# A decoder layer on one core: raw x transposed as it lands, the norm applied as a row, conditioning weights in smaller first pieces on three engines

## The chip, the cores and the metric

The kernel runs on one core of a Trainium2 chip. The metric is the device time of one execution in microseconds, the median of several runs. One run is also recorded by the hardware profiler; its span is the time from the first to the last recorded instruction. The engines are named as in the profile: PE (matrix products), PEld (its weight loads), DVE (vectors), ACT (scalar functions and copies), POOL (GpSimd) and SP, on whose queue nearly all DMAs of this kernel are issued.

## What is computed

One layer of a conditioned decoder with 512 positions and 1024 channels, in float32. Only its beginning is touched by the change: a norm without its gain, a modulation by a conditioning vector c, and the first columns of one wide projection. What follows (two attentions, an output projection, a gated MLP) stays.

```python
def rms_norm(x, gain):
    xf = x.astype(jnp.float32)
    y = xf * lax.rsqrt(jnp.mean(xf * xf, axis=-1, keepdims=True) + NORM_EPS)
    return (y * gain.astype(jnp.float32)).astype(x.dtype)
...
    mod = (jax.nn.silu(c) @ w_ada + b_ada)[:, None, :]
    shift_a, scale_a, gate_a, shift_f, scale_f, gate_f = jnp.split(mod, 6, axis=-1)

    h = rms_norm(x, attn_norm) * (1.0 + scale_a) + shift_a
    (nq, nkc, nvc, nks, nvs, nkw, nvw, ngate,
     cq, ckv, kr, bgate) = jnp.split(h @ w_in, IN_OFFSETS, axis=-1)
...
    x = x + gate_a * ((g_a * o_a + g_b * o_b) @ w_o)
    h = rms_norm(x, ffn_norm) * (1.0 + scale_f) + shift_f
...
    return x
```

## The kernel before

Products are kept exact in float32 by splitting each factor into a rounded high part and the rest: `split` (L82 to L84) makes the high part on ACT (L83) and the low part on DVE (L84), and `mm3` makes three matmuls on PE (L87), high by high, high by low, low by high. Names ending in h and l are such halves: wh and wl of a weight piece, hTh and hTl of h. PSUM banks go by letters, psG, psS, psT, psO, psF.

A tile framework orders the program. It takes instructions by a priority and by an estimate of when each can start, and then fixes a queue for each engine, which is worked off strictly in order; each DMA on SP's queue carries one of eight semaphores in turn, so that a DMA waits until the one eight places ahead has landed. The order within a queue is therefore the scheduler's and not that of the source.

The first stage (phase 1, from L409) goes so. x comes in eight pieces of 256 KB (L417). Each gives a sum of squares, on ACT (L437) or DVE (L434); two positions' sums at a time become 1/rms on POOL (`rstd`, L135). `x_half` (L444) scales x in place by that (ACT L447, DVE L449), transposes it on PE (L453) and copies the transposed piece xnT out of PSUM on ACT (L455). Channels then stand on partitions, in eight blocks of 128, k = 0 to 7.

For the modulation, `mod_acc(j)` (L462) loads, at every second j, eight pieces of w_ada of 256 KB, the shift and scale columns of two blocks, and adds them up, each times one entry per partition of silu(c), on DVE (`gemv_step`, L120 the first, L122 the others). `mod_cols` (L473) sums the result over partitions by a little matmul with ones (psT) and makes the columns mS (shift, L477) and mA (1 + scale times gain, L480).

`prep(k)` (L500) calls both, loads two pieces of w_in (408 and 384 columns, called wr1 and wr2), issues the late loads whose turn it is (`late_load`, L494; the table LATE says which go with which k), and makes h = xnT times mA plus mS on ACT (L507), hTh on ACT and hTl on DVE. The late loads are small tables for later: rowsB, the gain row of cq, tabs (832.5 KB), the gain row of ckv, rowg, cmp_w2, md (64 KB of the mask table), and two more rows. The k loop (L515) multiplies: for each k 12 matmuls of 408 columns into psG, psG, psS, psS and 9 of 512 columns into psO, psF and a psT. This is a k-step, named k0 to k7 below.

After the loop come the cq norm and gates (L539 to L552), a second group of columns (L555 to L565; again psG, psG, psS, psS and psF, which must be free first), the compressed-branch inputs kc and vc from psO, psF and psT (L569 to L582, products with tabs on DVE, which free those banks), and the compression. Two small DVE instructions that belong to later work are placed by the scheduler within this stage: rowg scaled (L617) and md cast into maskr (L619).

## Time and profile before

| what | value |
|---|---|
| device time, median of 3 runs | 950.85 us (950.5 to 951.32) |
| span of the profiled execution | 947.3 us |
| PE busy | 914.3 us (97%) |
| DVE busy | 690.8 us (73%) |
| ACT busy | 511.0 us (54%) |
| POOL busy | 51.1 us (5%) |
| moved by DMA | 113.06 MB, mean 119 GB/s |

Busy times are of the whole span; a share of it says little of a single stage, which is why the rows further down go by stretches and by single instructions. A timeline row gives start, length, engine, line, output and inputs, and in brackets how long the engine had stood idle and what released it. Matmuls are pipelined: the distance between two starts tells their pace better than their lengths do.

### The profile page before, as it was taken

What the parts mean: (1) busy time and instruction counts of PE and PEld (TensorE: products, weight loads), DVE (VectorE), ACT (ScalarE), POOL (GpSimd) and SP (SyncE); (2) the same over time, 40 slices, a digit from 0 to 9 for tenths busy, and PEclk for the clock granted to TensorE, in tenths of its full rate; (3) what the DMA queues carried; (4) which work ended last, traced back from release to release, by engine and by line L of the source; (5) the groups of instructions that cost most, each with busy time, mean ns of one, the idle gap of its engine ahead of it and who ended that gap; (6) DMA issues with size and microseconds to landing.
All of it is one profiled execution on the core that took longest, in us unless ns stands there. A gap on an engine that the chain in (4) does not pass through costs nothing.

```text
span 947.3 us, 15181 instructions
## 1 busy us (share of the span) xinstructions
PE 914.3 (97%) x5271; PEld 801.2 (85%) x5271; DVE 690.8 (73%) x1513; ACT 511.0 (54%) x1241; POOL 51.1 (5%) x57
## 2 busy tenths in 40 slices
PE   3999899999999999999999999999999999999998
PEld 2899788889889998888889899988888888888886
DVE  6967979787977779688967788797787666622423
ACT  5556758566676557558766655445444444422221
POOL 1000101001000001001001010000000000000000
PEclk9999999999999999999999999999999999999999
DMA  9945682441331253341214265263363333333421
GB/s 298 341 112 145 180 232 82 134 136 35 115 87 34 57 170 101 101 128 43 56 46 134 75 189 150 76 175 107 95 183 101 93 97 100 94 96 101 143 91 44
DMA packets 135778, 113.06 MB, mean 119 GB/s; under 512 B 7514, under 2 KB 118678, under 8 KB 135702
## 3 DMA queue, kind: packets, MB, share of 16 engines
q1 hardware_dynamic: 134934, 110.00, 39.4%
q0 software_dynamic: 768, 2.11, 0.7%
q8 instruction: 41, 0.67, 0.3%
q14 instruction: 35, 0.29, 0.1%
HBM read 109.98 MB, written 2.10 MB: 118 GB/s over the span
## 4 chain that ended last, share of the span: by engine, by line
PE 87%; ACT 4%; DVE 4%; DMA 3%; issue 1%; SPq 0%; POOL 0%; DVEq 0%; ACTq 0%
PE psG L87 43%; PE psS L87 23%; PE psO L87 8%; PE psF L87 4%; PE psT L87 4%; PE psT L783 2%; DMA wr<-in_w_in_dram 1%; DVE wl L84 1%; ACT Pt L760 1%; DMA wr<-in_cmp_v_w_dram 1%; ACT wh L83 1%; DMA ada<-in_w_ada_dram 1%; DMA x<-in_x_dram 1%; ACT sq L223 1%; PE psT L808 0%
## 5 line engine op out<-in xcount | busy, mean ns | idle before, releaser
L83 ACT ACTIVATE wh<-wr 128x512 fp32r<-128x512 f32 (+3 forms) x304 | 186.7, 621 | 289.5 <-PE psS L87 95.0
L84 DVE TENSOR_TENSOR wl<-wr,wh 128x512 fp32r<-128x512 f32 (+3 forms) x304 | 203.6, 676 | 155.4 <-ACT wh L83 148.4
L87 PE MATMUL psG<-hTh,wh 128*128 128x512 f32 x192 | 76.5, 398 | 1.0 <-DVE qr L328 1.0
L87 PE MATMUL psG<-hTh,wl 128*128 128x512 f32 x192 | 76.3, 397 | 0.1
L87 PE MATMUL psG<-hTl,wh 128*128 128x512 f32 x192 | 76.3, 397 | 0.0
L87 PE MATMUL psS<-h2l,wh 128*128 128x512 f32 (+1 forms) x184 | 68.3, 371 | 0.0
L87 PE MATMUL psS<-h2h,wl 128*128 128x512 f32 (+1 forms) x184 | 68.2, 371 | 0.0
L87 PE MATMUL psG<-h2h,wh 128*128 128x512 f32 (+1 forms) x184 | 68.2, 372 | 0.0
L87 PE MATMUL psG<-h2h,wl 128*128 128x512 f32 (+1 forms) x184 | 68.2, 371 | 0.0
L87 PE MATMUL psG<-h2l,wh 128*128 128x512 f32 (+1 forms) x184 | 68.1, 371 | 0.0
L87 PE MATMUL psS<-h2h,wh 128*128 128x512 f32 (+1 forms) x184 | 68.0, 370 | 0.0
L760 ACT ACTIVATE Pt<-psS,nm 128x128 f32<-128x128 f32 (+2 forms) x96 | 51.1, 534 | 25.8 <-DVE nm L755 20.1
L83 ACT ACTIVATE PTh<-psT 128x384 fp32r<-128x384 f32 (+1 forms) x72 | 36.5, 528 | 22.4 <-PE psT L783 22.2
L84 DVE TENSOR_TENSOR PTl<-psT,PTh 128x384 fp32r<-128x384 f32 (+1 forms) x72 | 42.1, 597 | 8.7 <-ACT PTh L83 8.1
L122 DVE SCALAR_TENSOR_TENSOR acc<-wr,csil,acc 128x512 f32<-128x512 f32 x60 | 44.8, 747 | 2.7 <-DMA wr<-in_w_ada_dram 1.5
L87 PEld LDWEIGHTS psG<-hTh,wh 128*128 128x128 f32 x192 | 36.2, 188 | 7.6 <-PE psS L87 0.7
L87 PEld LDWEIGHTS psG<-hTh,wl 128*128 128x128 f32 x192 | 36.1, 188 | 7.1 <-DVE wl L84 0.5
L87 PEld LDWEIGHTS psG<-hTl,wh 128*128 128x128 f32 x192 | 36.1, 188 | 6.4
L87 PE MATMUL psG<-wh,hTh 128*128 128x256 f32 (+2 forms) x128 | 37.5, 303 | 2.5 <-ACT hTh L83 1.4
L87 PEld LDWEIGHTS psG<-h2h,wl 128*128 128x128 f32 x184 | 34.7, 189 | 6.0
L87 PEld LDWEIGHTS psS<-h2l,wh 128*128 128x128 f32 x184 | 34.7, 189 | 6.0
L87 PEld LDWEIGHTS psS<-h2h,wh 128*128 128x128 f32 x184 | 34.7, 188 | 6.0
(431 smaller groups left out, 2593.8 us busy)
## 6 DMA issues: line engine op xcount, KB each, us to landing
wr<-in_w_up_dram SPq DMA_DIRECT2D x88, 256.0 KB, 3.0
wr<-in_w_ada_dram SPq DMA_DIRECT2D x64, 256.0 KB, 2.9
wr<-in_w_in_dram SPq DMA_DIRECT2D x48, 256.0 KB, 3.0
wr<-in_w_down_dram SPq DMA_DIRECT2D x44, 256.0 KB, 2.6
ada<-in_w_ada_dram SPq DMA_DIRECT2D x32, 256.0 KB, 5.4
wr<-in_w_o_dram SPq DMA_DIRECT2D x32, 256.0 KB, 3.0
wr<-in_w_in_dram SPq DMA_DIRECT2D x32, 128.0 KB, 3.6
wr<-in_cmp_k_w_dram SPq DMA_DIRECT2D x16, 256.0 KB, 3.7
```

The source lines that it names most:

```text
L83: act.activation(hi, src, AF.Copy)
L84: vec.tensor_sub(lo, src, f(hi))
L87: ins = pe.matmul(o, lhsT, rhs, start=start, stop=stop, skip_group_check=True)
L122: vec.scalar_tensor_tensor(acc, w, csil[:, k:k + 1], acc, op0=ALU.mult, op1=ALU.add)
L223: act.activation(sq[:, 0:n], b, AF.Square, accum_out=dst)
L760: act.activation(Pt[:, off[x2]:off[x2] + nt[x2]], Sb[x2], AF.Exp, bias=nm[:, x2:x2 + 1], scale=-1.0, accum_out=sums[:, x2:x2 + 1])
L783: pe.transpose(tr[:, e * P:(e + 1) * P], Pt[:, o:o + P], ident)
```

## The change

x is loaded column half first, and each transposed block is made from raw x as soon as its pieces have landed (`x_chunk`, into the banks T, S, G in turn). 1/rms is computed once for all positions, laid out as a row over positions, the same on every partition: four diagonal matrices times ones on PE, copied into rrow. h becomes xT times mA times rrow on DVE; hTh is its rounded sum with mS on ACT, and hTl the rest, on DVE.

The modulation goes by MOD_GROUPS. Blocks 0 and 1 get eight pieces of 128 KB each (rows of 512 bytes); the groups at 2, 4 and 6 keep eight pieces of 256 KB, of which the odd ones are scaled in place on ACT and added up on POOL, the even ones added up on DVE as before, and one DVE add joins the two. LATE sends rowsB, the cq row and tabs later. The code ahead of and behind this is as it was, with line numbers shifted (L617 and L619 are L636 and L638 after).

```diff
-LATE = (0, 1, 1, 1, 2, 2, 2, 3, 3, 4, 5, 6, 7, 8, 9, 9, 9)
-X_ACT = ((0, 0, 1, 1), (1, 1, 1, 1))
+LATE = (0, 0, 0, 0, 0, 1, 2, 2, 3, 3, 4, 5, 6, 7, 8, 9, 9)
+MOD_GROUPS = {0: 1, 1: 1, 2: 2, 4: 2, 6: 2}
...
-        x8 = [p1.tile([P, 4, 512], F32, name=f"x{t}", tag="x8", bufs=2) for t in range(2)]
-        xt = [[x8[t // 2][:, (t % 2) * 2 + i, :] for i in range(2)] for t in range(NT)]
+        x8 = [p1.tile([P, 4, 512], F32, name=f"x{i}", tag="x8", bufs=2) for i in range(2)]
         qs = [slot("q", f"qs{i}") for i in range(4)]
         rowsA = p1.tile([64, P], F32, name="rowsA")
         dma(rowsA, vec_a)
-        for t in range(NT):
-            for i in range(2):
-                dma(xt[t][i], x[t * P:(t + 1) * P, i * 512:(i + 1) * 512])
+        for i in range(2):
+            for t in range(NT):
+                dma(x8[i][:, t, :], x[t * P:(t + 1) * P, i * 512:(i + 1) * 512])
...
+        xT = []
+
+        def x_chunk(k):
+            tr = bank("TSG"[k % 3])
+            for t in range(NT):
+                pe.transpose(tr[:, t * P:(t + 1) * P], x8[k // 4][:, t, (k % 4) * P:(k % 4 + 1) * P], ident)
+            xk = slot("KV", f"xT{k}") if k < 6 else slot("KS", f"xT{k}")[:, 0:512]
+            act.activation(xk, tr, AF.Copy)
+            xT.append(xk)
...
+                if (t + i) % 2:
                     scr = pj.tile([P, 512], F32, name="scr", tag="t2")
-                    vec.tensor_tensor_reduce(scr, xt[t][i], xt[t][i], 1.0, 0.0, ALU.mult, ALU.add, ssh[:, t, i:i + 1])
+                    vec.tensor_tensor_reduce(scr, x8[i][:, t, :], x8[i][:, t, :], 1.0, 0.0, ALU.mult, ALU.add,
+                                             ssh[:, t, i:i + 1])
                 else:
                     scr = pj.tile([P, 512], F32, name="scr", tag="qg")
-                    act.activation(scr, xt[t][i], AF.Square, accum_out=ssh[:, t, i:i + 1])
-            if t % 2:
-                t2 = slice(t - 1, t + 1)
-                vec.tensor_add(ssx[:, t2], ssh[:, t2, 0], ssh[:, t2, 1])
-                rstd(rsx[:, t2], ssx[:, t2], D, [P, 2])
-        xnT = []
-
-        def x_half(i):
-            for t in range(NT):
-                if X_ACT[i][t]:
-                    act.activation(xt[t][i], xt[t][i], AF.Copy, scale=rsx[:, t:t + 1])
+                    act.activation(scr, x8[i][:, t, :], AF.Square, accum_out=ssh[:, t, i:i + 1])
+            for k in range(4 * i, 4 * i + 4):
+                x_chunk(k)
...
+        rsx = sm.tile([P, NT], F32, name="rsx")
+        rstd(rsx, ssx, D, [P, NT])
+        dg = pj.tile([P, 512], F32, name="dg", tag="qn")
+        for t in range(NT):
+            vec.tensor_scalar(dg[:, t * P:(t + 1) * P], ident, rsx[:, t:t + 1], None, op0=ALU.mult)
+        rb = bank("F")
+        for t in range(NT):
+            mm(rb[:, t * P:(t + 1) * P], ones, dg[:, t * P:(t + 1) * P], t == 0, True)
+        rrow = p1.tile([P, 512], F32, name="rrow")
+        vec.tensor_copy(rrow, rb)
...
+        def mod_acc(j):
+            if j not in MOD_GROUPS:
+                return
+            n = MOD_GROUPS[j]
+            w = 2 * n * P
+            accs = [slot("U", "acc")[:, 0:w], None]
+            first = [True, True]
+            for k in range(KD):
+                a = slot("ml", "ada")[:, 0:w]
+                dma(a.rearrange("p (s n) -> p s n", s=2),
+                    w_ada[k * P:(k + 1) * P, 0:2 * D].rearrange("p (s n) -> p s n", s=2)[:, :, j * P:(j + n) * P])
+                e = int(n > 1 and k % 2)
+                if e:
+                    act.activation(a, a, AF.Copy, scale=csil[:, k:k + 1])
+                    if first[e]:
+                        accs[e] = a
+                    else:
+                        pool.tensor_tensor(accs[e], accs[e], a, op=ALU.add)
                 else:
-                    vec.tensor_scalar(xt[t][i], xt[t][i], rsx[:, t:t + 1], None, op0=ALU.mult)
-            for k in range(4 * i, 4 * i + 4):
-                tr = bank("T")
-                for t in range(NT):
-                    pe.transpose(tr[:, t * P:(t + 1) * P], xt[t][i][:, (k % 4) * P:(k % 4 + 1) * P], ident)
-                xk = slot("KV", f"xnT{k}") if k < 6 else slot("KS", f"xnT{k}")[:, 0:512]
-                act.activation(xk, tr, AF.Copy)
-                xnT.append(xk)
-
-        x_half(0)
-
-        ACC = {}
-
-        def mod_acc(j):
-            if j % 2 == 0:
-                acc = slot("U", "acc")
-                for k in range(KD):
-                    a = slot("ml", "ada")
-                    dma(a.rearrange("p (s n) -> p s n", s=2),
-                        w_ada[k * P:(k + 1) * P, 0:2 * D].rearrange("p (s n) -> p s n", s=2)[:, :, j * P:(j + 2) * P])
-                    gemv_step(acc, a, k, True)
-                for i in range(2):
-                    ACC[j + i] = [acc[:, s * 256 + i * P:s * 256 + (i + 1) * P] for s in range(2)]
+                    gemv_step(accs[e], a, k, first[e])
+                first[e] = False
+            acc = accs[0]
+            if n > 1:
+                vec.tensor_add(acc, acc, accs[1])
+            for i in range(n):
+                ACC[j + i] = [acc[:, (s * n + i) * P:(s * n + i + 1) * P] for s in range(2)]
...
-            act.activation(h, xnT[k], AF.Identity, scale=mA[:, k:k + 1], bias=mS[:, k:k + 1])
+            vec.scalar_tensor_tensor(h, xT[k], mA[:, k:k + 1], rrow, op0=ALU.mult, op1=ALU.mult)
             hh, hl = slot("hT", f"hTh{k}", F32R), slot("hT", f"hTl{k}", F32R)
-            split(hh, hl, h)
+            act.activation(hh, h, AF.Identity, bias=mS[:, k:k + 1])
+            vec.scalar_tensor_tensor(hl, h, mS[:, k:k + 1], f(hh), op0=ALU.add, op1=ALU.subtract)
             hTh.append(hh)
             hTl.append(hl)
 
         prep(0)
-        x_half(1)
```

The change moves instructions on the engines as the scheduler decides. Three places follow. The numbers in the names are the program's, they differ from kernel to kernel.

DVE around h of k6: before, in a row (wr_597 and wr_603 are the pieces of w_in for k6, wr_644 and wr_650 those for k7; hTl_613 is that of k6, hTl_659 that of k7).

```order
L480 TENSOR_TENSOR mA<-bp,colA 128x1
L84 TENSOR_TENSOR wl<-wr_597,wh 128x408
L84 TENSOR_TENSOR wl<-wr_603,wh 128x384
L84 TENSOR_TENSOR hTl_613<-h,hTh_612 128x512
L617 TENSOR_SCALAR rowg<-rowg 128x64
L477 TENSOR_TENSOR mS<-psT,colA 128x1
L479 SCALAR_TENSOR_TENSOR bp<-psT,colA 128x1
L480 TENSOR_TENSOR mA<-bp,colA 128x1
L619 CAST maskr<-qs_113 128x128
L84 TENSOR_TENSOR wl<-wr_644,wh 128x408
L84 TENSOR_TENSOR hTl_659<-h,hTh_658 128x512
L84 TENSOR_TENSOR wl<-wr_650,wh 128x384
```

DVE at the same place after the change (wr_634 and wr_640 are the pieces for k6, wr_680 those for k7; xT_198 and hTl_649 are of k6).

```order
L84 TENSOR_TENSOR wl<-wr_634,wh 128x408
L636 TENSOR_SCALAR rowg<-rowg 128x64
L496 TENSOR_TENSOR mS<-psT,colA 128x1
L498 SCALAR_TENSOR_TENSOR bp<-psT,colA 128x1
L84 TENSOR_TENSOR wl<-wr_640,wh 128x384
L499 TENSOR_TENSOR mA<-bp,colA 128x1
L638 CAST maskr<-qs_113 128x128
L526 SCALAR_TENSOR_TENSOR h<-xT_198,mA,rrow 128x512
L529 SCALAR_TENSOR_TENSOR hTl_649<-h,mS,hTh_648 128x512
L84 TENSOR_TENSOR wl<-wr_680,wh 128x408
```

The cast of md (L619, now L638) stood behind hTl of k6, and now stands ahead of h of k6, which has come to DVE.

ACT around hTh of k1: before (wr_362 and wr_368 are the pieces for k2; h<-xnT_177 and hTh_304 are of k1).

```order
L83 ACTIVATE wh<-wr_290 128x408
L83 ACTIVATE wh<-wr_296 128x384
L83 ACTIVATE wh<-wr_362 128x408
L507 ACTIVATE h<-xnT_177,mS,mA 128x512
L83 ACTIVATE wh<-wr_368 128x384
L83 ACTIVATE hTh_304<-h 128x512
L507 ACTIVATE h<-xnT_184,mS,mA 128x512
```

ACT at the same place after the change (wr_390 and wr_396 are the pieces for k2; the L478 are scalings of odd pieces of w_ada, those around hTh_328 of group 4; hTh_328 is of k1, hTh_404 of k2).

```order
L478 ACTIVATE ada<-ada,csil 128x512 x3
L83 ACTIVATE wh<-wr_314 128x408
L83 ACTIVATE wh<-wr_320 128x384
L83 ACTIVATE wh<-wr_390 128x408
L478 ACTIVATE ada<-ada,csil 128x512 x2
L83 ACTIVATE wh<-wr_396 128x384
L528 ACTIVATE hTh_328<-h,mS 128x512
L478 ACTIVATE ada<-ada,csil 128x512 x2
L528 ACTIVATE hTh_404<-h,mS 128x512
```

Ahead of hTh of k1 there are now the scalings of two pieces of the group that is needed for k4 and k5; h is no longer in this queue.

SP around the first pieces: before (wr_232 and wr_238 are the pieces of w_in for k0, wr_290 to wr_368 those for k1 and k2).

```order
L417 DMA x_112<-in_x_dram 128x512 x4
L467 DMA ada<-in_w_ada_dram 128x2x256 x8
L112 DMA wr_232<-in_w_in_dram 128x408
L112 DMA wr_238<-in_w_in_dram 128x384
L494 DMA rowsB<-in_vec_b_dram 76x128
L467 DMA ada<-in_w_ada_dram 128x2x256 x8
L112 DMA wr_290<-in_w_in_dram 128x408
L112 DMA wr_296<-in_w_in_dram 128x384
L112 DMA wr_362<-in_w_in_dram 128x408
L112 DMA wr_368<-in_w_in_dram 128x384
```

SP at the same place after the change (wr_264 and wr_270 are the pieces of w_in for k0, wr_314 to wr_396 those for k1 and k2).

```order
L416 DMA x_112<-in_x_dram 128x512 x4
L474 DMA ada<-in_w_ada_dram 128x2x128 x16
L474 DMA ada<-in_w_ada_dram 128x2x256
L112 DMA wr_264<-in_w_in_dram 128x408
L474 DMA ada<-in_w_ada_dram 128x2x256
L112 DMA wr_270<-in_w_in_dram 128x384
L474 DMA ada<-in_w_ada_dram 128x2x256 x6
L112 DMA wr_314<-in_w_in_dram 128x408
L112 DMA wr_320<-in_w_in_dram 128x384
L112 DMA wr_390<-in_w_in_dram 128x408
L112 DMA wr_396<-in_w_in_dram 128x384
L474 DMA ada<-in_w_ada_dram 128x2x256 x8
```

The pieces of w_in for k0 now stand behind sixteen half-size pieces and one or two full ones of w_ada.

## Rows read from the trace of the kernel before

**Rows 1.** Page, busy time and share of the span: PE and the others
```profile
PE 914.3 (97%) x5271; PEld 801.2 (85%) x5271; DVE 690.8 (73%) x1513; ACT 511.0 (54%) x1241; POOL 51.1 (5%) x57
```

**Rows 2.** Busy us by stretch, then granted clock, DMA share, GB/s (engines as named)
```profile
core 0: us, PE busy (x) PEld busy (x) DVE busy (x) ACT busy (x) POOL busy (x), PEclk, DMA share, GB/s
0.00:25.00 25.00, 10.40 (x45) 8.13 (x46) 17.63 (x45) 14.43 (x29) 3.04 (x8) 1.00 0.93 302
25.00:30.00 5.00, 4.66 (x28) 4.15 (x27) 4.72 (x13) 3.23 (x6) 0.00 (x0) 1.00 1.09 351
10.00:45.00 35.00, 28.34 (x140) 24.52 (x140) 32.83 (x72) 21.24 (x38) 1.70 (x2) 1.00 1.07 347
0.00:50.00 50.00, 33.64 (x167) 29.27 (x168) 39.16 (x96) 27.64 (x51) 3.04 (x8) 1.00 0.98 320
50.00:55.00 5.00, 5.00 (x29) 4.62 (x28) 1.73 (x7) 1.20 (x3) 0.00 (x0) 1.00 0.55 151
```

**Rows 3.** Timeline of PE: start, us, line, output and inputs, [idle before <-releaser]
```profile
29.73 0.46 PE L87 MATMUL psG<-wh,hTh 128*128 128x408 f32 x1
...
45.04 0.45 PE L87 MATMUL psG<-wh,hTh 128*128 128x408 f32 x1 [1.41 <-ACT hTh L83]
...
54.62 0.34 PE L87 MATMUL psG<-wh,hTh 128*128 128x408 f32 x1
...
58.88 0.34 PE L87 MATMUL psG<-wh,hTh 128*128 128x408 f32 x1
...
70.98 0.50 PE L87 MATMUL psF<-hTh,wh 128*128 128x512 f32 x1 [0.35 <-DVE a L575]
```

**Rows 4.** Timeline of DVE at the late small loads
```profile
54.09 0.20 DVE L617 TENSOR_SCALAR rowg<-rowg 128x64 f32<-128x64 f32 x1 [2.46 <-DMA rowg<-in_row_g_dram]
...
54.97 0.23 DVE L619 CAST maskr<-qs 128x128 bf16<-128x128 f32 x1 [0.37 <-DMA qs<-in_tab_dram]
```

**Rows 5.** Instructions by line and shape, 0 to 60 us: busy us, mean ns of one
```profile
L122 DVE SCALAR_TENSOR_TENSOR acc<-ada,csil,acc 128x512 f32<-128x512 f32 x28 | 21.0, 749 | 0.7 <-DMA ada<-in_w_ada_dram 0.3
...
L507 ACT ACTIVATE h<-xnT,mS,mA 128x512 f32<-128x512 f32 x8 | 6.5, 810 | 6.8 <-DVE mA L480 4.3 <-DVE hTl L84 2.4
...
L83 ACT ACTIVATE hTh<-h 128x512 fp32r<-128x512 f32 x8 | 5.0, 624 | 0.1
...
L83 ACT ACTIVATE wh<-wr 128x384 fp32r<-128x384 f32 x8 | 4.1, 517 | 1.2 <-DMA wr<-in_w_in_dram 0.6 <-PE psT L87 0.6
...
L447 ACT ACTIVATE x<-x,rsx 128x512 f32<-128x512 f32 x6 | 3.9, 712 | 2.8 <-POOL rsx L135 2.8
```

**Rows 6.** DMA queue: packets, MB, share of 16 engines, 68 to 70 us (512-byte rows)
```profile
q1 hardware_dynamic: 511, 0.25, 48.9%
```

**Rows 7.** The same, 11 to 17 us (conditioning weights, rows of 1 KB)
```profile
q1 hardware_dynamic: 2106, 2.14, 109.2%
```

**Rows 8.** SP's queue, waits of 0 to 60 us: total, times, longest
```profile
SPq L494 <- DMA tabs<-in_tab_dram: 2.4, 1, 2.4
```

**Rows 9.** Timeline of POOL
```profile
1.02 0.29 POOL masks.py:199 TENSOR_SCALAR_AFFINE_SELECT ident<-ident 128x128 f32<-128x128 f32 x1
...
106.42 1.02 POOL L135 TENSOR_TENSOR r<-ms,neghalf 128x4 f32<-128x4 f32 x1 [20.10 <-DVE ms L132]
113.31 2.59 POOL L135 TENSOR_TENSOR r<-ms,neghalf 128x4 f32<-128x4 f32 x1 [5.88 <-DVE ms L132]
```

**Rows 10.** Timeline of DVE beside the operation at 113.31
```profile
113.13 0.70 DVE L84 TENSOR_TENSOR wl<-wr,wh 128x512 fp32r<-128x512 f32 x1
...
114.33 0.70 DVE L84 TENSOR_TENSOR wl<-wr,wh 128x512 fp32r<-128x512 f32 x1
114.94 0.29 DVE L650 SCALAR_TENSOR_TENSOR th<-th,psT 128x128 f32<-128x128 f32 x1
```

More of the change, by code (lines that the diff above doesn't have):

```diff
@@ L118, in gemv_step @@
     def gemv_step(acc, w, k, init):
-        if k == 0 and init:
-            vec.tensor_scalar(acc, w, csil[:, 0:1], None, op0=ALU.mult)
+        if init:
+            vec.tensor_scalar(acc, w, csil[:, k:k + 1], None, op0=ALU.mult)
         else:
@@ L127, in gemv @@
             dma(w, w_ada[k * P:(k + 1) * P, c0:c0 + 512])
-            gemv_step(acc, w, k, init)
+            gemv_step(acc, w, k, init and k == 0)
     def rstd(o, ss, n, shape):
@@ L433, in tile_hybrid_layer @@
+        ssh = sm.tile([P, NT, 2], F32, name="ssh")
+        for i in range(2):
+            for t in range(NT):
+                if (t + i) % 2:
                     scr = pj.tile([P, 512], F32, name="scr", tag="t2")
-                    vec.tensor_tensor_reduce(scr, xt[t][i], xt[t][i], 1.0, 0.0, ALU.mult, ALU.add, ssh[:, t, i:i + 1])
+                    vec.tensor_tensor_reduce(scr, x8[i][:, t, :], x8[i][:, t, :], 1.0, 0.0, ALU.mult, ALU.add,
+                                             ssh[:, t, i:i + 1])
@@ L460, in tile_hybrid_layer @@
+        rb = bank("F")
+        for t in range(NT):
+            mm(rb[:, t * P:(t + 1) * P], ones, dg[:, t * P:(t + 1) * P], t == 0, True)
+        rrow = p1.tile([P, 512], F32, name="rrow")
+        vec.tensor_copy(rrow, rb)
         ACC = {}
         def mod_acc(j):
[L463 to L471 removed]
+            if j not in MOD_GROUPS:
[15 more added lines that the diff above has]
+                        pool.tensor_tensor(accs[e], accs[e], a, op=ALU.add)
+                else:
+                    gemv_step(accs[e], a, k, first[e])
[5 more added lines that the diff above has]
+                ACC[j + i] = [acc[:, (s * n + i) * P:(s * n + i + 1) * P] for s in range(2)]
```

8 lines of the change are left out of this document (2 added, 6 removed).

## The prediction

> **What bounds the kernel now.** I read the page's busy shares first: PE is busy 97% of the span [rows 1]. So the question is never how much work DVE or ACT has in all, but where PE waits, and whether a later start of the first stage's PE work is made good anywhere. The changed instructions all lie in the first 75 us, so I went next to stretches of that time. In the first 50 us the DMA engines are full (16.0 MB at 320 GB/s, share 0.98) and DVE is busy 39 of 50 us; from 50 us the loads thin out (151 GB/s) and DVE has 1.7 us of work in 5, while PE is busy 5.00 of 5.00 [rows 2]. So until 50 us loads and DVE set the pace, and PE after that.
>
> Third, PE's timeline at the first matmul of a k-step, the psG<-wh,hTh one. k1 starts at 29.73, k4 at 45.04 after a gap of 1.41, k6 at 54.62, k7 at 58.88; PE next waits at 70.98, for 0.35, at the F bank of the second group [rows 3]. k1 to k6 is 24.89 us, 23.5 without the gap, 4.7 a step with the little matmuls of the conditioning between; k6 to k7 is 4.26; k7 to the F bank 12.10. Behind the F bank the two kernels queue the same instructions in the same order on PE, which is full, so a shift of that matmul is a shift of the end. The forecast is therefore the start of k6 and k7 afterwards, and what the second group adds.
>
> Fourth, what stands in front of h and hTh on DVE and ACT. Before, DVE stood 2.46 us for rowg (54.09) and 0.37 for the small table md (the cast at 54.97) [rows 4]. Nothing on PE noticed: these stand between hTl of k6 and the work of k7, and ACT makes h.
>
> **The change part by part.**
>
> *Raw x transposed, norm as a row.* Six scalings of x on ACT (0.71 each) and two on DVE go [rows 5], and the transposes no longer wait for the norm. Four small diag products, four matmuls and a copy come. All of it lies ahead of k0. k0 needs its own two w_in pieces, which now stand behind sixteen half-size and one or two full conditioning pieces. It may start a little earlier than before; I give it no value, since PE then waits for k1 anyway, and 4.3 us of k0 end well ahead of that.
>
> *Smaller first pieces.* 2.10 MB now come in rows of 512 bytes. In a stretch that moved 0.25 MB in 511 packets the queue was busy 48.9% of 16 engines for 2 us, 30.6 ns a packet; in one of 1 KB packets 2106 took 109.2% of 6 us, 49.8 ns [rows 6, 7]. Two halves cost 61.2 against 49.8, and 2048 of them over 16 engines 1.46 us: every load behind is 1.5 us later. Lower bound 0 (halves at half the price). The total of bytes up to md stays the same.
>
> *k1.* On ACT, hTh of k1 now stands behind two scalings of group 4's pieces and the wh that follows (order list). Ahead of the fourth piece of group 4 stand x, the first three groups, three steps of w_in and four pieces, 2.10+2.10+2.10+1.22+1.05 = 8.57 MB; before, 7.55 MB had moved by 25 us and 351 GB/s followed [rows 2], so byte 8.57 is at 27.9, and with the 1.5 at 29.4. Then a scaling 0.71, wh 0.52 and hTh 0.62 [rows 5] and small gaps: k1 at 31.5, 1.8 us later than before. From there at 23.5 us to k6: 55.0, if nothing else holds.
>
> *h on DVE, and the loads of md.* This is the term that decides. h for a step costs 0.75 on DVE in place of 0.81 on ACT, hTl keeps its form [rows 5]; eight steps are balanced by half of the conditioning products leaving DVE, so as a sum of work this is nothing. But the order list has h of k6 on DVE directly behind the cast that waits for md, and rowg a few instructions ahead of it. A DMA that no PE work depended on until k7 now stands ahead of k6. What is queued behind the cast: h, hTl, both wl of k7, its columns and its h; who waits: hTh of k6 on ACT, then PE.
>
> When does md land? Before, at about 54.95. Byte-bound: what moved in 50 to 55 us is 0.755 MB, 2.2 us at 350 GB/s, so 52.2 and with the slower halves 53.7. At the old pace with the halves on top: 56.5. The old pace had SP stand 2.4 us until the big table tabs had landed [rows 8]; now tabs is issued later, after the w_in of k7, and the small loads follow it directly, so that wait should go but tabs lands later. I take the middle, 55.1, for want of a row that decides. Then cast 0.23, h 0.75, hTh 0.62 and three hand-overs of about 0.05: k6 at 56.85, against 54.62: **+2.23**. It hides a k1 as late as 33.3 (56.85 less 23.5), so the 1.8 of k1 costs nothing more, and the old 1.41 gap ahead of k4 may come or go without effect. For md at 53.7 and 56.5 the term is +0.8 and +3.6.
>
> k7 follows k6 by 4.26: from md DVE needs cast, h, hTl, two wl, columns and h, some 4 us, and hTh another 0.65, while PE has 1.75 + 4.26 = 6.0 us from md.
>
> *Second group.* In k7 all products with hTh now come first and those with hTl after, so psO closes after 12 matmuls of 0.185 and 5 of 0.227 (a step is 12 and 9 of them, 4.26), at 3.35 us, where 12 and 3 made 2.9. DVE's products with the tables on psO and psF end the wait of the F bank, and DVE is back to back from there. **+0.45**; at best 0, if the banks that close together let DVE run on.
>
> Sum: span 947.3 + 2.23 + 0.45 = 950.0. The median of the runs lies 3.55 us above this span, so the time is **953.5**.
>
> *POOL's adds.* Nine new 128x512 adds, three in each of groups 2, 4 and 6, then one DVE add that waits for them. No row shows such an add; a 128x128 select took 0.29 on POOL, four times that is 1.17, an estimate [rows 9]. Three of them lie beside DVE's own four products of 0.75 and the loads, so in the sum I set them at nothing. The Trainium skill, page "GPSIMD Engine Reference", section "3.1 Elementwise — side-by-side cycle accounting", gives 4497 ns for an add of 2048 elements; a quarter of that, an estimate from that page, is 1.12 us, and the sum by it would be the same. If the cover is gone this becomes a rival, below.
>
> **The rivals.**
>
> *A: POOL and DVE shut each other out.* At 113.31 a small POOL operation took 2.59 us, where the same one took 1.02 at 106.42. Over it DVE ran three two-input operations on SBUF back to back (0.70 each, the first at 113.13, the last at 114.33), then one that reads PSUM at 114.94; 113.31 + 2.59 = 115.90 is 0.96 after that, the operation's own length [rows 9, 10]. So POOL got nothing until DVE let go. DVE's conditioning products, its wl, h and hTl are nearly all of that kind, and DVE is busy 33 of the 35 us from 10 to 45 [rows 2]. Then a group's adds, 3 x 1.17 = 3.5 us, run only when DVE stands still for them. In group 2 that puts h of k1 3.5 us back, k1 at 35.0 and k6 at 58.5, 1.65 above the forecast. Two steps of DVE work per later group are 0.48 + 3 x 0.75 + 0.69 + 2 x 3.1 = 9.6 us, 13.1 with the adds, against 2 x 4.7 on PE: one such pair uncovered adds 3.7. So 955.2 to 958.9, say 957. Against it: from 45 us DVE has room, and it waits for loads between pieces. The Trainium skill, page "SBUF — State Buffer", section "Who interferes with whom", says a DVE instruction with two SBUF inputs contends with a GpSimd instruction that reads SBUF, and that the one that comes second fully blocks; the row at 113.31 agrees (2.59 against 1.02).
>
> *B: no change.* md lands byte-bound at 53.7 and the banks close in time: 947.3 + 0.8 + 0 to 0.45 + 3.55 = 951.7 to 952.1. For it: the loads were full before 50 us. Against: the last small loads must still queue behind 0.85 MB of tabs.
>
> *C: faster.* One mechanism: the loads of the second half run ahead. If ACT's scalings and POOL's adds free the conditioning buffers earlier, so that SP is never held, and the halves cost nothing, k1 would start at 28 and md land by 50.5, a saving of the old 1.41 gap as well: k6 at 51.5 to 52.2, 2.4 to 3.1 earlier, time 948 to 949. It decides only if md lands before about 52.4 (k6 at 54.2 or earlier). Against it: 16.7 MB at 350 GB/s do not fit in ahead of that.
>
> *D: only k0 and k1 matter.* If the scheduler's order did not bind, that is md landed early but ACT's scalings hold each hTh as at k1, k6 would be at 55.0 to 56, 951.7 to 952.7; it is not told apart from B by the time.
>
> Of the clock: the granted clock is 1.00 in all these rows [rows 2], so no row prices a lower one; k0 at twice its length would still end ahead of k1.
>
> **How the numbers follow.** About 0.2%, 1.9 us, is what a measurement of this kernel can tell from no change: same is 948.95 to 952.75. The forecast, k6 behind md, 952.2 to 955.2 round 953.5: 0.45, of which a tenth lies in same. A: 0.20, all slower. B and D: 0.25, same for the greater part. C: 0.08, mostly faster. Something worse in the same direction (loads as late as 56.5 and contention): 0.02. That makes faster 0.08, same 0.28, slower 0.64. The range reaches down past B to 950.3 and up into A to 957.5.
>
> **What would show it.** Right: DVE's cast waits at about 55 for qs<-in_tab, its h for k6 follows, and PE has a gap of 1.5 to 2.5 us ahead of k6 that ends with hTh; k1 at 31 to 32; the F bank 12.5 us behind k7. A would show POOL's adds far over 1.2 us and DVE's add on two accumulators (L488) waiting for POOL for microseconds. B would show md landed by 54. Wrong altogether: a gap ahead of k6 that ends with another releaser, or none; a k1 as late as 35; or PE's later work shifting by another amount than the F bank.

## The result and the profile after

The changed kernel takes 958.08 us (median of 4 runs, 957.54 to 958.45), the kernel before 950.67 beside it; the ratio of the runs on record is 1.0083, with a 95% interval of 1.0069 to 1.0097 (the two medians alone give 1.0078). It is slower by 7.4 us, where 2.7 were forecast, and the time lies 0.6 us above the range.

PE's timeline of the changed kernel, at the first matmul of a k-step and at the second group, which answers to [rows 3] (start, us, line, output and inputs, [idle before <-releaser]):

```profile
22.86 0.71 PE L87 MATMUL psG<-wh,hTh 128*128 128x408 f32 x1 [3.49 <-ACT hTh L528]
...
35.17 0.71 PE L87 MATMUL psG<-wh,hTh 128*128 128x408 f32 x1 [1.94 <-ACT hTh L528]
...
41.39 0.34 PE L87 MATMUL psG<-wh,hTh 128*128 128x408 f32 x1
...
52.49 0.46 PE L87 MATMUL psG<-wh,hTh 128*128 128x408 f32 x1 [1.62 <-ACT hTh L528]
...
61.99 0.44 PE L87 MATMUL psG<-wh,hTh 128*128 128x408 f32 x1
...
71.98 0.38 PE L87 MATMUL psG<-wh,hTh 128*128 128x320 f32 x1 [0.95 <-ACT sq L563]
```

Set beside the kernel before, with the F bank and the first matmul of the compression (psO) behind it:

| start, us | k0 | k1 | k2 | k3 | k4 | k6 | k7 | second group | F bank | compression |
|---|---|---|---|---|---|---|---|---|---|---|
| before | 23.50 | 29.73 | 34.13 | 38.40 | 45.04 | 54.62 | 58.88 | 63.17 | 70.98 | 83.63 |
| after | 22.86 | 35.17 | 41.39 | 46.01 | 52.49 | 61.99 | 66.43 | 71.98 | 79.68 | 92.22 |
| later by | -0.64 | 5.44 | 7.26 | 7.61 | 7.45 | 7.37 | 7.55 | 8.81 | 8.70 | 8.59 |

Three steps make nearly the whole of it: 5.4 us up to k1, 1.8 from k1 to k2, and 1.3 between k7 and the second group. Of the 1.8, 1.29 is the pace of k1's first eight matmuls (2.88 us up to the first psO product, 1.59 before), and 0.36 a little matmul pair of the conditioning that now lies within this step. From k2 to k7 only 0.3 is added; the old gap of 1.41 ahead of k4 is there again, as 1.62. The span grows from 947.3 to 955.8, as much as the compression is late, so the shift is handed on to the end.

k1 waited for hTh, and hTh on ACT for h, which is DVE's now. ACT's row of it, then DVE's and POOL's timelines around h of k1:

```profile
34.39 0.72 ACT L528 ACTIVATE hTh<-h,mS 128x512 fp32r<-128x512 f32 x1 [2.15 <-DVE h L526]
```

```profile
24.42 4.90 DVE L122 SCALAR_TENSOR_TENSOR acc<-ada,csil,acc 128x256 f32<-128x256 f32 x3
...
30.20 0.68 DVE L488 TENSOR_TENSOR acc<-acc,ada 128x512 f32<-128x512 f32 x1
...
32.36 0.14 DVE L496 TENSOR_TENSOR mS<-psT,colA 128x1 f32<-128x1 f32 x1
...
32.60 0.97 DVE L499 TENSOR_TENSOR mA<-bp,colA 128x1 f32<-128x1 f32 x1
33.60 0.75 DVE L526 SCALAR_TENSOR_TENSOR h<-xT,mA,rrow 128x512 f32<-128x512 f32 x1
...
36.20 1.25 DVE L499 TENSOR_TENSOR mA<-bp,colA 128x1 f32<-128x1 f32 x1
...
39.95 0.69 DVE L488 TENSOR_TENSOR acc<-acc,ada 128x512 f32<-128x512 f32 x1 [1.18 <-POOL ada L482]
```

```profile
23.79 4.98 POOL L482 TENSOR_TENSOR ada<-ada 128x512 f32<-128x512 f32 x3 [9.52 <-ACT ada L478]
31.91 1.65 POOL L482 TENSOR_TENSOR ada<-ada 128x512 f32<-128x512 f32 x1 [3.14 <-DMA ada<-in_w_ada_dram]
35.86 4.06 POOL L482 TENSOR_TENSOR ada<-ada 128x512 f32<-128x512 f32 x2 [2.31 <-DMA ada<-in_w_ada_dram]
...
45.70 3.00 POOL L482 TENSOR_TENSOR ada<-ada 128x512 f32<-128x512 f32 x2 [2.85 <-DMA wr<-in_w_in_dram]
```

A row merges neighbours under the first one's shape: at 24.42 it is one product of 128x256 (0.48 where nothing disturbs it) and two of 128x512 (0.75 [rows 5]), which together took 4.90 us while POOL made its first three adds in 4.98. An operation on 128 single numbers (mA, L499) took 0.97 and 1.25, where it takes 0.15 undisturbed; the first of them ends at 33.57, together with POOL's add (31.91 and 1.65 make 33.56). mS, one of whose inputs lies in PSUM, took 0.14 beside the same add. Of POOL's nine adds the seven that ran in a pair or a three took 1.5 to 2.0 each. The columns of k1 come late on DVE (mS at 32.36): in its queue they stand behind all of group 2 (the joining add at 30.20) and two products of group 4.

Granted clock and load by stretch (busy us and instructions of PE, PEld, DVE, ACT, POOL, then PEclk, DMA share, GB/s):

```profile
15.00:20.00 5.00, 2.71 (x12) 2.35 (x11) 4.47 (x14) 0.54 (x1) 0.00 (x0) 0.50 1.00 291
20.00:25.00 5.00, 2.14 (x6) 2.10 (x7) 4.42 (x10) 3.01 (x5) 1.21 (x1) 0.50 1.07 354
25.00:30.00 5.00, 5.00 (x20) 4.28 (x19) 4.96 (x5) 2.75 (x6) 3.61 (x3) 0.71 1.09 362
30.00:35.00 5.00, 0.79 (x5) 0.52 (x4) 4.93 (x11) 2.01 (x4) 1.65 (x1) 0.98 1.09 359
35.00:40.00 5.00, 4.83 (x19) 4.61 (x20) 3.82 (x9) 2.52 (x5) 3.98 (x2) 0.68 1.07 335
```

PE was at half clock from 15 to 27.9 us, and again for k1's first 2.9 us after it had stood 4.4 of the 5 us ahead of it. Before, [rows 2] show 1.00 throughout.

The operation on which the forecast rested, DVE's cast of md, and rowg:

```profile
57.12 0.19 DVE L636 TENSOR_SCALAR rowg<-rowg 128x64 f32<-128x64 f32 x1
...
58.09 0.22 DVE L638 CAST maskr<-qs 128x128 bf16<-128x128 f32 x1
58.22 0.74 DVE L526 SCALAR_TENSOR_TENSOR h<-xT,mA,rrow 128x512 f32<-128x512 f32 x1
```

Neither row has a wait: the tables had landed when DVE came to them, and PE was busy until 61.99 with k5. So the order was as read, h of k6 behind the cast, but the term was worth nothing.

### The profile page after: what moved, and what is told of

It reads as the page before. It is cut to its first block, busy times and chain, and to the rows that moved or that the text cites. A ratio compares the mean times of both kernels' runs of the same rounds, so it can differ in the third digit from the quotient of the medians.

```text
span 955.8 us, 15218 instructions
## 1 busy us (share of the span) xinstructions
PE 920.0 (96%) x5279; PEld 806.3 (84%) x5279; DVE 699.4 (73%) x1521; ACT 509.4 (53%) x1239; POOL 64.4 (7%) x65
## 4 chain that ended last, share of the span: by engine, by line
PE 86%; DVE 5%; ACT 4%; DMA 3%; issue 1%; POOL 0%; SPq 0%; DVEq 0%; ACTq 0%; POOLq 0%
PE psG L87 42%; PE psS L87 23%; PE psO L87 8%; PE psF L87 4%; PE psT L87 4%; PE psT L802 2%; DMA ada<-in_w_ada_dram 1%; DVE wl L84 1%; DVE acc L122 1%; DMA wr<-in_cmp_v_w_dram 1%; ACT Pt L779 1%; ACT wh L83 1%; ACT sq L223 1%; DMA x<-in_x_dram 0%; PE psT L827 0%
## 5 line engine op out<-in xcount | busy, mean ns | idle before, releaser
L87 PEld LDWEIGHTS psG<-h2h,wh 128*128 128x128 f32 x184 | 34.6, 188 | 6.0
```

Of the source, the lines that this page charges most:

```text
L87: ins = pe.matmul(o, lhsT, rhs, start=start, stop=stop, skip_group_check=True)
```

## The experiments

All times stand against the kernel before on the same chip, 949.9 to 950.1 us in these sets. The changed kernel was timed beside one of 950.67, so a difference between it and a run below is known to about 0.7 us only. The first diffs are against the changed kernel, and where one is against another, the text says so.

### The adds taken from POOL, and the split taken out

```diff
-                        pool.tensor_tensor(accs[e], accs[e], a, op=ALU.add)
+                        vec.tensor_tensor(accs[e], accs[e], a, op=ALU.add)
```

> The changed kernel with the nine adds of the odd, ACT-scaled conditioning pieces on DVE instead of POOL; nothing else edited. Theory 'shut out' (a POOL add and DVE's two-input operations block each other): in the changed kernel DVE operations were stretched by 3.6 us (three products of 128x256 took 4.90), 2.8 us (three tiny products of 128x1 at about 1.0 each), 1.0 and 1.0, and DVE waited 1.18 for POOL, 9.7 us in all; nine adds of 0.69 on DVE cost 6.2, so h of k4 should come some 3 us earlier, at about 48, no DVE operation of 128x512 should exceed 0.8 us, and the time should be about 955. Rival 'ACT queue' (hTh stands behind the scalings): unchanged, 957 to 958. Rival 'clock' (PE at half pace in k0 and part of k1 is what delays): unchanged, 957 to 958.

Measured 960.18 us, ratio 1.0106 (1.009 to 1.0121): a miss for all three. No DVE operation is stretched any more, but k1 is at 36.99 and k4 at 53.03. DVE makes the same sum itself, and every odd piece now goes through ACT first and comes back into DVE's queue:

```profile
24.83 0.69 DVE L482 TENSOR_TENSOR ada<-ada 128x512 f32<-128x512 f32 x1
...
26.09 0.68 DVE L482 TENSOR_TENSOR ada<-ada 128x512 f32<-128x512 f32 x1
...
32.84 0.75 DVE L122 SCALAR_TENSOR_TENSOR acc<-ada,csil,acc 128x512 f32<-128x512 f32 x1 [0.61 <-DMA ada<-in_w_ada_dram]
33.51 0.68 DVE L482 TENSOR_TENSOR ada<-ada 128x512 f32<-128x512 f32 x1
34.11 0.15 DVE L499 TENSOR_TENSOR mA<-bp,colA 128x1 f32<-128x1 f32 x1
...
35.44 0.74 DVE L526 SCALAR_TENSOR_TENSOR h<-xT,mA,rrow 128x512 f32<-128x512 f32 x1
```

Here mA of k1 (34.11) stands behind a product that waited 0.61 for its load and the add behind that. The work on DVE ahead of h is what counts, and where it stands, not only whether POOL disturbs it.

```diff
-                e = int(n > 1 and k % 2)
+                e = 0
```

> The changed kernel without the split of groups 2, 4 and 6: every piece by the multiply-add on DVE, no scaling on ACT, no add on POOL. Theory 'shut out': DVE has twelve multiply-adds of 0.75 in place of nine adds on POOL and three on DVE, like the run with the adds on DVE; 954 to 956, with h of k4 at about 48. Rival 'ACT queue': hTh of k1 no longer stands behind scalings, so this one should beat the run with DVE adds by 2 us or more, 951 to 953. Rival 'clock': unchanged, 957 to 958.

(The joining add goes with it.) Measured 955.79, ratio 1.0066 (1.0048 to 1.0085): inside "shut out"; "ACT queue" had the difference to the run with DVE's adds right and the time wrong. k1 is at 35.66, no earlier than in the changed kernel, but k4 at 50.97 without a wait. It beats the run with DVE's adds by 4.4 us: the way through ACT costs by itself, but it isn't the reason for k1. Nor are POOL's adds alone, since there are none here.

### A fill in place of each add

```diff
-                        pool.tensor_tensor(accs[e], accs[e], a, op=ALU.add)
+                        pool.memset(accs[e], 0.0)
```

> The changed kernel with each of the nine POOL adds replaced by a fill of the same 128x512 tile on POOL: same engine, same place in the queues but for a few rows, it writes SBUF and reads none. The odd pieces' products so stay out of the modulation. Theory 'shut out': DVE's two-input operations are stretched because POOL reads SBUF beside them; here the three products of 128x256 at the place where they took 4.90 us take 1.3, h of k1 comes 3 to 4 us earlier (k1 at 31 to 32.5 against 35.17), k4 without its gap or earlier, time 952 to 955. Rival 'order': k1 is late because its columns stand behind two later groups' work on DVE, whatever POOL does: k1 at 34 or later, 957 to 958.

This kernel leaves the sums of the odd pieces out. Measured 954.92, ratio 1.0056 (1.004 to 1.0071), 3.2 us less than the changed kernel, or 2.5 if each is taken against its own kernel before (7.4 and 4.9). DVE's order up to k1 is the same but for one add. Its timeline at the same place, and POOL's fills of group 4:

```profile
25.02 1.93 DVE L122 SCALAR_TENSOR_TENSOR acc<-ada,csil,acc 128x256 f32<-128x256 f32 x3
...
31.66 0.15 DVE L496 TENSOR_TENSOR mS<-psT,colA 128x1 f32<-128x1 f32 x1
...
31.91 0.16 DVE L499 TENSOR_TENSOR mA<-bp,colA 128x1 f32<-128x1 f32 x1
32.10 0.75 DVE L526 SCALAR_TENSOR_TENSOR h<-xT,mA,rrow 128x512 f32<-128x512 f32 x1
...
56.02 0.20 DVE L636 TENSOR_SCALAR rowg<-rowg 128x64 f32<-128x64 f32 x1 [2.18 <-DMA rowg<-in_row_g_dram]
```

```profile
30.94 1.69 POOL L482 MEMSET ada<- 128x512 f32 x3 [7.06 <-ACT ada L478]
```

The three products take 1.93 in place of 4.90, mA 0.16 in place of 0.97. k1 comes 1.5 us earlier (33.66), later than "shut out" and earlier than "order" had it, and k4 3.1 earlier (49.41, no gap). These are two different readings. No fill lies beside the three products (those of group 2 ran at 22.20, before them), so they show what DVE does without POOL beside it. mA and h at 31.91 and 32.10 do lie beside fills, and they are not stretched.

The fills are also shorter, run as soon as the first odd piece is scaled, and let the other pieces' buffers go without being read, so the 2.5 to 3.2 us are not those of the reading of SBUF alone. But DVE had waited for POOL's result only 1.18 us in the changed kernel; most of the gain is stretched operations. Ahead of h of k1 they had cost 2.97 and 0.81, and only 1.5 came back, since DVE got there 0.6 later (25.02) and then stood 0.58 and 0.60 for pieces of w_ada. What is left at k1, 33.66 against 29.73, is not POOL's; its columns still stand behind group 2 and two products of group 4, as "order" has it, but no run here shows the order to be the whole cause.

### Each part of the change by itself

The split of the groups at 2, 4 and 6 over ACT and POOL, put into the kernel before:

```diff
+                    if j and k % 2:
+                        act.activation(a, a, AF.Copy, scale=csil[:, k:k + 1])
+                        if odd is None:
+                            odd = a
+                        else:
+                            pool.tensor_tensor(odd, odd, a, op=ALU.add)
+                    else:
+                        gemv_step(acc, a, k, True)
+                if odd is not None:
+                    vec.tensor_add(acc, acc, odd)
```

> The kernel before with one part of the change alone: in the conditioning groups at 2, 4 and 6 the odd pieces are scaled on ACT and added on POOL, one DVE add joins them. Theory 'shut out': DVE is released of 12 multiply-adds (9.0 us) and gets 3 adds (2.1), but is stretched and made to wait by up to 9.7 us; k4 no earlier than before (45.0) and perhaps 3 us later; 950.5 to 954, and stretched DVE operations at the POOL adds. Rival 'ACT queue': h and hTh are both on ACT here, behind scalings: 953 to 956 without stretched DVE operations. If the split did what it is for, k4 without its gap: 949.

Measured 955.12, ratio 1.0052 (1.0037 to 1.0067): the dearest part, 1.1 above "shut out" and inside "ACT queue", which had said that no DVE operation would be stretched. k1 is at 32.08 and k2 at 38.74, 6.66 us apart where it was 4.40, and then there is no wait up to k7 (62.05). The waits ahead of k1 end with DVE, not with ACT, and DVE shows the same stretching:

```profile
22.95 1.36 DVE L84 TENSOR_TENSOR hTl<-h,hTh 128x512 fp32r<-128x512 f32 x1 [0.44 <-ACT hTh L83]
24.23 1.78 DVE L122 SCALAR_TENSOR_TENSOR acc<-ada,csil,acc 128x512 f32<-128x512 f32 x1
...
33.61 1.23 DVE L490 TENSOR_TENSOR mA<-bp,colA 128x1 f32<-128x1 f32 x1
...
36.41 1.13 DVE L120 TENSOR_SCALAR acc<-ada,csil 128x512 f32<-128x512 f32 x1 [0.30 <-DMA ada<-in_w_ada_dram]
```

hTl takes 1.36 for 0.69, a product 1.78 for 0.75, mA 1.23 for 0.15, and the first product of a group, which has one input tile and a column, 1.13 for 0.48. The granted clock by 2 us:

```profile
28.00:30.00 2.00, 0.87 (x6) 0.43 (x4) 1.97 (x8) 0.82 (x3) 0.00 (x0) 1.00 1.10 355
30.00:32.00 2.00, 1.15 (x8) 1.06 (x7) 1.97 (x6) 2.00 (x4) 0.52 (x1) 0.56 1.07 361
32.00:34.00 2.00, 2.00 (x8) 1.95 (x8) 1.75 (x5) 0.82 (x2) 1.92 (x2) 0.50 1.08 366
34.00:36.00 2.00, 2.00 (x7) 1.78 (x6) 2.00 (x3) 1.78 (x3) 0.88 (x2) 0.50 1.09 361
36.00:38.00 2.00, 2.00 (x9) 1.79 (x8) 1.70 (x3) 1.82 (x4) 1.26 (x1) 0.73 1.08 359
```

Two gaps of 1.13 and 0.85 us stand ahead of k1 (PE busy 2.02 of 4 us), and the clock was at half for most of the 6 us behind them.

Raw x, the norm as a row and h on DVE, with the modulation and LATE of the kernel before (against the changed kernel):

```diff
-LATE = (0, 0, 0, 0, 0, 1, 2, 2, 3, 3, 4, 5, 6, 7, 8, 9, 9)
+LATE = (0, 1, 1, 1, 2, 2, 2, 3, 3, 4, 5, 6, 7, 8, 9, 9, 9)
...
-            n = MOD_GROUPS[j]
...
+            if j % 2 == 0:
...
                 dma(a.rearrange("p (s n) -> p s n", s=2),
-                    w_ada[k * P:(k + 1) * P, 0:2 * D].rearrange("p (s n) -> p s n", s=2)[:, :, j * P:(j + n) * P])
-                e = int(n > 1 and k % 2)
+                        w_ada[k * P:(k + 1) * P, 0:2 * D].rearrange("p (s n) -> p s n", s=2)[:, :, j * P:(j + 2) * P])
+                    gemv_step(acc, a, k, k == 0)
```

> The changed kernel with the conditioning and the late loads of the kernel before: raw x transposed as it lands, norm as a row, h on DVE, but full first pieces and all conditioning on DVE. Theory 'shut out': POOL does nothing here, DVE carries h (8 x 0.75) on top of the old load and loses the two scalings, so k4 is 1 to 3 us later than before: 951 to 954. Rival 'clock': PE idle ahead of k0 as in the changed kernel, half pace in k0, 952 to 955. If the x part is worth something by itself: 949 or less. The second group starts some 1.3 us later after k7 than before if that comes from the order of k7's products (all hTl last).

Measured 952.94, ratio 1.003 (1.002 to 1.0041), inside "shut out" and inside "clock". It starts k0 at 25.31 and k1 at 32.50, and h on DVE fills that engine. From 20 to 45 us, this kernel and then the kernel before (columns as above):

```profile
20.00:45.00 25.00, 20.82 (x94) 19.15 (x95) 24.93 (x56) 7.79 (x14) 0.00 (x0) 0.79 1.05 341
```

```profile
20.00:45.00 25.00, 23.21 (x121) 20.86 (x121) 24.06 (x56) 13.84 (x24) 0.00 (x0) 1.00 1.06 345
```

DVE is busy 24.93 of 25 us where it had 24.06, and ACT 7.79 where it had 13.84. So h, 0.75 a step, moved from an engine with room to the one without. The clock of 0.79 says that PE also ran part of this at half speed. The timeline divides the two: k0 starts 1.81 us later than before, k0 to k1 takes 7.19 in place of 6.23 with no wait ahead of k1 (its first matmuls are 0.34 apart, 0.185 before), and from k1 to the second group the two kernels take 33.52 and 33.44. All of it lies ahead of k1, then, up to 1 us of it in PE's pace; the later steps' h cost nothing. The second group stands 4.29 behind k7, as in the kernel before: the order of k7's products did not change here.

The smaller pieces, put into the kernel before:

```diff
-            if j % 2 == 0:
-                acc = slot("U", "acc")
+            n = {0: 1, 1: 1, 2: 2, 4: 2, 6: 2}.get(j)
+            if n:
+                w = 2 * n * P
+                acc = slot("U", "acc")[:, 0:w]
...
-                        w_ada[k * P:(k + 1) * P, 0:2 * D].rearrange("p (s n) -> p s n", s=2)[:, :, j * P:(j + 2) * P])
+                        w_ada[k * P:(k + 1) * P, 0:2 * D].rearrange("p (s n) -> p s n", s=2)[:, :, j * P:(j + n) * P])
```

> The kernel before with the first two conditioning groups in half-size pieces (eight of 128 KB for k0, eight for k1) and nothing else. It makes 16 products of about 0.42 on DVE out of 8 of 0.72, so 1 us more DVE work ahead of k1, and moves the weights of k0 behind 2 MB of conditioning instead of 2 MB plus nothing; k0 no earlier than 22, k1 1 to 3 us later than 29.73 if DVE's order puts later groups ahead of k1's columns again. Theory 'DVE and order': 951 to 953. Rival 'half-size rows are slow' (1.5 us on every load): k4 also 1.5 later, 951.5 to 952.5, with DVE waiting for loads. If the smaller pieces help as such: 949.

Measured 952.45, ratio 1.0026 (1.0015 to 1.0036). k0 is at 25.44, k1 at 32.78, k4 at 46.54. The two theories are not told apart by the time; DVE waited 1.7 us for pieces that begin a group, where it waited 0.3 before, so both have their share. But k7 is only 1.62 late and the second group 2.88: the other 1.26 is the order of k7's products, which the scheduler changed here too, with the same wait of 0.95 for ACT's squares. The run with the split has it as well (3.17 at k7, 4.41 at the second group). In the changed kernel itself the queue's row from 11 to 17 us is 31.0 ns a packet of 512 bytes (16 engines by 6 us by 1.141 over 3528), against 49.8 for 1 KB in [rows 7]:

```profile
q1 hardware_dynamic: 3528, 1.72, 114.1%
```

The three parts alone cost 5.2, 3.0 and 2.5 us, 10.7 together, and all at once 7.4 to 7.9. By the start of the compression they are 4.18, 2.20 and 2.65 late, 9.0 together against 8.59, and two of them hold the 1.26 of k7's order, which the whole has once. So by the traces the parts come to the whole within 1 us, and by the times they come to 3 us more; how much of that is waits of one part that cover waits of another is not shown.

### The order of DVE, the clock, the order of k7

DVE's order, in the changed kernel:

```diff
+        keep = tc.keep_in_program_order
...
-                    gemv_step(accs[e], a, k, first[e])
+                    keep(gemv_step(accs[e], a, k, first[e]))
```

(The joining add, mS and h are held to the written order in the same way.)

> The changed kernel with DVE's conditioning held in written order: all of a step's products, its columns and its h ahead of the next group's products. In the changed kernel the columns of k1 stand behind two groups' products. Theory 'order': k1 at 27 to 30 in place of 35.17, the granted clock no longer falls between k0 and k1, k2 to k4 then set by the conditioning's loads and POOL's adds; 953 to 956. Rival 'shut out decides everything': POOL's adds take the same time from DVE, only later; k1 early, but k4 at 52 or later, 957 to 958.

Measured 973.59, ratio 1.0248 (1.0234 to 1.0262), and k1 at 37.77: a clear miss for both. Put ahead, the columns of k1 make DVE stand for what the other engines have not made yet, and DVE's products are not done in those pauses:

```profile
23.88 0.16 DVE L496 TENSOR_TENSOR mS<-psT,colA 128x1 f32<-128x1 f32 x1 [1.17 <-PE psT L87]
...
25.87 0.75 DVE L529 SCALAR_TENSOR_TENSOR hTl<-h,mS,hTh 128x512 fp32r<-128x512 f32 x1 [0.79 <-ACT hTh L528]
...
34.23 1.37 DVE L84 TENSOR_TENSOR wl<-wr,wh 128x408 fp32r<-128x408 f32 x1 [2.79 <-ACT wh L83]
...
35.97 0.75 DVE L526 SCALAR_TENSOR_TENSOR h<-xT,mA,rrow 128x512 f32<-128x512 f32 x1
```

So written order is no cure; the scheduler's order filled DVE's pauses.

The clock, in the kernel before with the split (twelve extra matmuls behind k0, into columns of the G and S banks that it leaves unused):

```diff
+            if k == 0:
+                for i in range(12):
+                    mm(bA[i % 4][:, 408:512], f(hl[:, 0:P]), f(w1l[:, 0, 0:104]), False, False)
```

> The kernel before with the split alone (as in e3_before_split), and twelve small matmuls more at the end of k0, into columns of the banks that nobody reads, so that PE does not stand still for 1.1 us ahead of k1. Theory 'clock': in e3_before_split the granted clock fell to 0.50 from 31 us after two gaps of 1.13 and 0.85, and k1 to k2 took 6.66 in place of 4.40; with the gap filled it stays at 1.00, k1 to k2 is 4.4 to 4.6 and the time 952.5 to 953.5 against 955.1. Rival: the matmuls only shift k0's end and DVE's lateness stays the limit, 955 to 956.

Measured 954.67, ratio 1.0049 (1.0036 to 1.0063), between the two expected ranges and not to be told from 955.12. The granted clock is shown as 1.00 from 15 to 50 us, and k1 to k2 took 5.15 (k2 at 38.12) in place of 6.66. But k1 itself came later, at 32.97, and not by a wait: PE had no pause ahead of it. The extra matmuls took 2.6 us of its time, and k0's first eight followed one another at 0.34 us, the pace of k0 in the changed kernel, though the clock column shows 1.00 there; why, stays open. New waits for hTh stood ahead of k3 (0.61) and k4 (1.29). So this run moved k1 as well as the clock, and the price of the clock at the end of this kernel is not shown; in the changed kernel, where k4 waits 1.62 for h, it stays open too.

The order of k7, in the changed kernel:

```diff
-                mm3(bA[t][:, 0:408], hh[:, ts], hl[:, ts], w1h[:, 0, :], w1l[:, 0, :], st, sp)
+                mm3(bA[t][:, 0:408], hh[:, ts], hl[:, ts], w1h[:, 0, :], w1l[:, 0, :], st, sp, sp)
```

(mm3 of psO, psF and psT in the same way; the last argument holds the order, in k7 alone.)

> The changed kernel with the matmuls of k7 held in the order in which they are written (high, low, low products of one bank after the other, as PE did them before). In the changed kernel the second group starts 5.55 us after k7, with a wait of 0.95 for ACT's squares of the first G bank, against 4.29 before. Theory 'banks close late': 4.3 to 4.6, the time 956.8 to 957.2. Rival 'later work takes it back' (the F bank is set by DVE's products with the tables): start of the second group earlier, but the F bank no earlier, 958.

Measured 957.27, ratio 1.0077 (1.0063 to 1.0091), 0.8 us less than the changed kernel, or 0.2 if each is taken against its own kernel before: no difference by the time. The trace shows the mechanism: k7 at 66.59, the second group at 70.98, 4.39 behind it in place of 5.55, and the wait for ACT's squares is gone; the compression starts at 90.83 in place of 92.22. How much of that 1.39 reaches the end is not shown.

### What the kernel before had to give

ACT's order from the first step on, in the kernel before:

```diff
+            PIN[0] = True
             wk[k] = (load_w([(w_in, O_NG, 408)], k, 1, slot("cq", "wr1")),
...
+            tc.keep_in_program_order(act.activation(h, xnT[k], AF.Identity, scale=mA[:, k:k + 1], bias=mS[:, k:k + 1]))
```

(While PIN is set, `split` holds its ACT instruction as well.)

> Not the change, but the kernel before with one thing: ACT's instructions of a k-step held in written order, so that h and hTh of k4 do not stand behind the two weight pieces of k5, whose loads they waited for (gap of 1.41 ahead of k4 at 45.04). If that gap is ACT's order: k4 at 43.2 to 43.7, time 949.3 to 949.8 against about 950.5. If DVE or the loads of k4 set it anyway: no difference.

Measured 949.18, ratio 0.9991 (0.9982 to 0.9999): 0.9 us less than the kernel before, the only version here that is faster than the kernel before, and hardly clear of its own noise. k4 comes at 43.71 with a wait of 0.29 instead of 1.41, so the gap was ACT's order. k7 is 1.24 earlier and the second group is where it was (63.18), with a wait of 0.94 for the G bank.

The same with the order of k7 held as well, that is, the diffs of these two runs together:

> Not the change: the kernel before with ACT's order held as in b1_before_pinact and the matmuls of k7 in written order as in e5_k7_order. b1 had k7 1.24 us earlier and lost it at the second group, which waited 0.94 for ACT's squares of the first G bank (63.18 against 63.17). Theory 'banks close late': the second group at 62.0, time 947.9 to 948.4. Rival 'later work takes it back' (F bank set by DVE): 949 to 949.5.

Measured 949.84, ratio 0.9998 (0.9989 to 1.0006), above both expectations. The second group starts at 62.11 and the compression at 81.97, 1.66 earlier than before, and the time is the same. PE's waits and the granted clock behind it:

```profile
99.24 0.50 PE L91 MATMUL psS<-wh,hTh 128*128 128x256 f32 x2 [0.58 <-ACT wh L85]
...
106.10 0.50 PE L91 MATMUL psG<-wh,hTh 128*128 128x256 f32 x2 [0.70 <-ACT wh L85]
107.25 0.39 PE L91 MATMUL psG<-wl,hTh 128*128 128x256 f32 x1 [0.65 <-DVE wl L88]
```

```profile
104.00:108.00 4.00, 2.65 (x19) 2.13 (x18) 3.96 (x8) 3.59 (x12) 1.02 (x1) 1.00 0.56 163
108.00:112.00 4.00, 4.00 (x24) 4.00 (x23) 4.00 (x8) 3.03 (x10) 0.23 (x1) 0.57 0.41 131
```

The gain met weights that were not split any earlier, PE stood for wh and wl, and 4 us at a clock of 0.57 followed. The kernel before stands at the same matmuls, for 0.44, 0.63 and 0.72, and its clock stays at 1.00. At 128 us the two kernels are level (128.19 here for the matmul that starts at 128.10 before).

## Why the prediction was wrong

*Direction and where to look: right.* The first 75 us decide, and here a later F bank is a later end: 8.70 at the F bank, 8.59 at the compression, 8.5 in the span. The mechanism that was to make it later was wrong, and a k1 as late as 35, one of the signs of that, came.

*POOL's adds "set at nothing": the step that failed.* They were priced as if they lay beside DVE's products. Beside them is where they cost most. Rival A had the mechanism and the place, and the row at 113.31 in [rows 9] that shows it was in hand; a chance of 0.20 was too little for the only direct row on the matter. The fill run puts POOL's adds at 2.5 to 3.2 us of the 4.6 by which the forecast was short. Rival A's own time, 957, lies 1.1 short, and its k1 (35.0 forecast, 35.17 measured) is in part luck: it had all of the 3.5 us from the adds, where the fill run gives them 1.5 there and the rest at k4, and without any work on POOL k1 was at 35.66.

*k1 at 31.5: mis-sized by 3.7 us.* The step followed ACT's queue (scalings, then hTh) and the loads. hTh waited 2.15 us for h, on DVE: there the columns of k1 stand behind group 2 and two pieces of group 4, which the sum didn't go through. Even with the fills k1 was at 33.66.

*h on DVE "as a sum of work nothing": not enough.* The sum over the stage is level; over the 25 us in which DVE is the bound it is not. The x part by itself costs 3.0 us, all of it ahead of k1: 1.81 in a later k0, which had been given no value, and the rest in k0 itself.

*h of k6 behind md, +2.23: nothing.* The order was right, but md had landed before DVE came to it, since k6 was by then late for other reasons. The term hung on k1 hiding under it (up to 33.3), and k1 did not. It was covered, not absent: md was issued at 50.00 and took 6.8 us to land, so it came at about 56.8, later than the 55.1 taken, and cast, h and hTh behind it would have let k6 start at about 58.6 (an estimate from 0.22, 0.74 and 0.72 and the hand-overs), where it started at 61.99. In the fill run DVE does stand 2.18 for rowg there, and PE comes to k6 at 58.93 without a wait.

*Half-size pieces, 1.5 us on every load: size right* (31.0 ns a packet against 30.6 forecast), and 2.5 us by themselves in the time, through DVE's extra instructions and k7's order too.

*Second group, +0.45: 1.26.* The sum looked at psO and the F bank. It was the G banks: with all hTl last they close with the 12th and 13th matmul of k7 in place of the 5th and 6th, and PE must wait for ACT's squares of the first (0.95). Holding the order gives 1.16 of it back on PE.

*The clock "no row prices": incomplete.* The half clock came where PE stood ahead of k0, as the remark allowed, and costs nothing there, since PE stood again ahead of k1. It came again behind that wait, and k1 to k2 took 6.22 in place of 4.40, 1.29 of it by the pace of the first eight matmuls. That it can fall in the middle of the loop was a rival that I did not set up.

*Span to time.* The 3.55 us around the span were taken from a median. In the sets beside the experiments the time of the kernel before lies 1.8 to 2.2 us above the span of the same execution, and executions with a span of 947.3 took 949.2 to 949.3. So the profiled execution of before was a short one, some 1.5 below its median, while that of the changed kernel (957.54, span 955.8) is 0.5 below its own: that is the 1 us between a shift of 8.5 by the spans and of 7.4 by the medians. The forecast of the shift doesn't depend on it.

## What to carry to other kernels

Before work is handed to POOL to relieve DVE, look at what DVE runs meanwhile: if it is two-input work on SBUF, the two engines took turns here, and tiny operations of the chain were held about as long as large ones. A bound engine is relieved by what leaves its queue ahead of the awaited instruction, so walk that queue to the instruction itself, and count a moved operation (h) against the engine it comes to within the stage that binds. The loss ahead of a full PE was handed on whole here (8.59 us at the compression, 8.5 in the span); a gain of 1.66 at the same place was lost by 128 us.
